# Four matmuls per block of rows: both high-part products first, then both low-part ones

## The chip, the core and the metric

The kernel runs on one core of one Trainium2 chip. The metric is the device time of one execution in microseconds (us). Most of the work is matrix multiplication on TensorE; ScalarE (ACT in the profile) and VectorE (DVE) prepare the weights and finish results, and DMA queues bring the weights from memory.

## What is computed

Two transformer blocks run on 256 tokens of 2048 features, all in float32. The first has gated linear attention, a gated convolution and a feed-forward layer; the second has a layer of pooled features and one of attention with low-rank keys and queries. Nearly all of the arithmetic is products of the activations with weight matrices:

```python
proj = jnp.einsum('bsd,dn->bsn', h, w_in[l])
...
x = x + jnp.einsum('bsd,de->bse', merged, w_o[l])
h2 = rms_norm(x, g_ffn[l])
hid = jnp.square(jax.nn.relu(jnp.einsum('bsd,df->bsf', h2, w_ffn_up[l])))
x = x + jnp.einsum('bsf,fd->bsd', hid, w_ffn_down[l])
```

## The kernel before

The activations are kept transposed, features on the 128 partitions and the 256 tokens along the free dimension. To multiply in float32 precision with the faster float32r type, each operand is written as a sum of two float32r parts, a high one and a low one. The product is taken as high x high, plus high weight x low activation, plus low weight x high activation.

Weights stream in blocks of 1 MB, in an order written out by hand (`weight_order`, L58). Each block is two units of 512 KB. For each unit `ensure` (L254) issues one ScalarE instruction that writes the high part `wh` and one VectorE instruction that writes the low part `wl`, three units ahead of their use (`NLOOK`); the next block's DMA is issued on SP's queue. At the end of each unit `end_unit` (L324) lets small tasks step: evacuation of finished sums, norms, attention pieces. Those tasks bring their own small matmuls, which stand between units on TensorE.

The function `group` (L358) is where most matmuls come from. It computes 512 output columns: two PSUM tiles, each with two feature tiles of 128 columns, and for each feature tile the 256 tokens twice, side by side: one half collects the products with the high activations (and later the low weights), the other those with the low activations. A unit holds four blocks of 128 rows (`k`, 0 to 3) of the weights for two feature tiles (`f`, 0 and 1). For each `k` and `f` the loop issues a long matmul (stationary `wh`, moving 512 columns: both parts of the activations) and a short one (stationary `wl`, moving 256 columns: the high part alone), each with its own weight load (LDWEIGHTS). So a unit has 8 long and 8 short matmuls. The helper `mm` (L227) records every matmul, so all of them carry line L230.

Three places do similar work and are not edited: the branch of `group` for a single block of 512 rows (`n == 1`, three short matmuls for each `k` and `f`), `group_tok` (L419, tokens on the partitions, where the weights are the moving operand, all matmuls 512 columns) and `narrow` (L438, one block of 128 columns).

Of the kernel before, what the change touches and what calls it, by code (L numbers as in the profile page):

```python
# [18 lines left out]
P = 128  # L19
# [38 lines left out]
def weight_order():  # L58
    """The order in which 1 MB weight blocks are used: (array, group of output columns, block of rows)."""
    out = []  # L60

    def add(name, groups, kbs=range(NKB)):
        for g in groups:
            out.extend((name, g, kb) for kb in kbs)

    add("q", range(2))
    add("lr", [0], [0])
    add("k", range(2))
    add("v", range(4))
    for g in range(4):  # L70
        for name in ("cc", "cx", "cb"):
            add(name, [g])
    for g in range(4):
        add("gb", [g])
        add("conv_out", [g])
    add("r", range(4))
    for g in range(4):
        add("ga", [g])
        add("gla_out", [g])
    add("o", range(4))  # L80
    for part in range(4):
        add("up", range(4 * part, 4 * part + 4))
        add("down", range(4), range(4 * part, 4 * part + 4))
    for half in range(2):
        for gi in (2 * half, 2 * half + 1):
            add("u", (2 * gi, 2 * gi + 1))
            add("pgate", (2 * gi, 2 * gi + 1))
            add("pgroup", (2 * gi, 2 * gi + 1), range(2))
        add("pout", range(4), range(4 * half, 4 * half + 4))
    add("kva", [0])  # L90
    add("kvr", [0], [0])
    add("qa", [0])
    for name, g in MLA:
        add(name, [g], range(NKB) if name == "bgate" else [0])
    add("bout", range(4))
    return out
# [3 lines left out]
def kernel(  # L100
# [29 lines left out]

    # ---------------------------------------------------------------- storage
    class Slot:
        """A tile in one of a fixed number of equal places, held until free()."""

# [42 lines left out]

    # ---------------------------------------------------------------- short names
    def wide(r, n=4):
        return r.unsqueeze(1).to_broadcast([r.shape[0], n, r.shape[-1]])  # L180

    # Estimated work given to each engine so far, in ns: paces the tasks between the units.
    spent = {"PE": 0.0, "DVE": 0.0, "ACT": 0.0}
# [47 lines left out]

    # ---------------------------------------------------------------- weight stream
    order = weight_order()
# [20 lines left out]
    def ensure(u, between=None):  # L254
        """Split the weights up to unit u into two float32r parts whose sum is the float32 value."""
        while state["split"] <= min(u, len(units) - 1):
# [18 lines left out]

    # ---------------------------------------------------------------- tasks between the units
    tasks = []
# [57 lines left out]
    class Out:  # L335
        """A result in SBUF, complete after `left` calls of put()."""

# [20 lines left out]
    def group(name, g, rhs, kbs=range(NKB), into=None):  # L358
        """The 512 output columns of group g, [128 features, 4, 256 tokens]: two PSUM tiles of 2 feature tiles,
        with the products of the two parts of the activations side by side. The sum of the parts goes to a slot,  # L360
        or, feature tile by feature tile, to into(ps, first feature tile)."""
        kbs = list(kbs)
# [24 lines left out]
        for e, (sb, i) in enumerate(seq):  # L387
            if sb not in acc:
                acc[sb] = psum_now("main", (P, 2, 2, T))
            ps = acc[sb]  # L390
            wh, wl = next_unit(name, g, kbs[e // 2])
            x = rhs(i)
            for k in range(4):
                first, last = i == 0 and k == 0, i == n - 1 and k == 3
                for f in range(2):
                    cs = slice(f * P, (f + 1) * P)
                    mm(ps[:, f], wh[:, k, cs], x[k // 2][:, k % 2], first, False)
                    mm(ps[:, f, 0, :], wl[:, k, cs], x[k // 2][:, k % 2, 0, :], False, last)
            end_unit()
            if i == n - 1:  # L400
                def fold(ps=ps, sb=sb):
                    fs = slice(2 * sb, 2 * sb + 2)
                    if into is None:
                        out.put(lambda s: fold_parts(s[:, fs, :], ps))
                    else:
                        out.put(lambda s: into(ps, fs))
                    ps.done()

                if into is not None:
                    out.make = lambda: 0  # L410
                defer(fold)
# [7 lines left out]
    def group_tok(name, g, rhs, kbs=range(NKB)):  # L419
        """PSUM tile [128 tokens, 2, 512 features]: the same product, tokens on the partitions."""  # L420
        ps = psum_now("main", (P, 2, 512))
# [16 lines left out]
    def narrow(name, rhs):  # L438
        """Row tile [128 features, 256 tokens] of one 128-column block."""
        ps = psum_now("misc", (P, 1, 2, T))  # L440
# [16 lines left out]

    # ---------------------------------------------------------------- splits and norms
    class Pair:
        """Groups of 4 feature tiles as two float32r parts whose sum is the float32 value: a group is two slots  # L460
        [128, feature tile, part, 256]."""

# [10 lines left out]
        def halves(self, i):  # L473
            """(feature tiles, high part, high part as float32, low part) of each slot."""
            return [(slice(2 * a, 2 * a + 2), s[:, :, 0, :], s.t.bitcast(F32)[:, :, 0, :], s[:, :, 1, :])
# [25 lines left out]
    class SumSq:  # L501
        """Sum of squares over 4 feature tiles at a time, still one for each partition."""

# [35 lines left out]
    def rstd_steps(out, m, mean_plus_eps):  # L539
        """out = 1 / sqrt(m), m already holding the mean plus eps; one Newton step."""  # L540
        mean_plus_eps()
# [8 lines left out]
    def spread(out, c):  # L550
        """out[p, t] = c[t]: the column [128 tokens, 2] as a row on all partitions."""
        dg = row("dg")
# [10 lines left out]
    def token_sums(ss):  # L563
        """PSUM [128 tokens, 2]: the sums of squares of the tokens."""
        tot = ss.fold()
# [8 lines left out]
    def rms_steps(ss, n, out, c):  # L574
        """The norm's factor of each token, as a column c and as a row out."""
        ps = yield from token_sums(ss)
# [13 lines left out]

    # ---------------------------------------------------------------- constants
    ones = const.tile([P, P], F32, name="ones")
# [26 lines left out]
    rows = {}  # L619
# [3 lines left out]

    # ================================================================ first block
    h = Pair(4)
# [33 lines left out]
    def decay(ps_lr):  # L659
        """log of the decay of each token and key feature, summed within blocks of 128 tokens."""  # L660
        wg = slot("wg", (P, 1024))
# [32 lines left out]

    # scores of the gated linear attention, a level of the token tree at a time
    ST = []
# [136 lines left out]

    # gated convolution
    cbu = Pair(4)
# [96 lines left out]
    for n in ("R16", "R2"):  # L932
        rows.pop(n).free()
    # the residual stream again
    xs = [slot("x") for _ in range(4)]
# [29 lines left out]

    # feed-forward
    gfa = const.tile([P, 16], F32, name="gfa")
# [33 lines left out]
    def two_norms():  # L1001
        """The final norm of the first block, then the first norm of the second on its result."""
        r1, r2 = row("R1"), row("R12")
# [32 lines left out]

    # ================================================================ second block
    hkv, hb = Pair(4), Pair(4)
# [20 lines left out]
    def pool_evac(ps, gi, n, pooled):  # L1059
        """Mean over the last tokens, less the token itself."""  # L1060
        while "R12" not in rows:
# [58 lines left out]

    # rotary tables
    trig = [row("C"), row("S")]
# [27 lines left out]

    # keys, values, queries
    rope_task = spawn(rope_tables())
# [19 lines left out]
    def rope_rows(out, raw, n):  # L1172
        """raw: [128, n, 256], two heads of 64 features on the partitions."""
        ps = yield from psum_later("misc", (P, n, T))
# [131 lines left out]
    def attend(hq):  # L1306
# [6 lines left out]
        begun[hq] = state["unit"]  # L1313
        # factor of the scores: 192^-0.5 times the norm of the queries
        rq = rows["Cq"]
# [115 lines left out]

# [1 line left out]
def _blocks(name, w):  # L1433
    """[K, N] -> [N/512, K/512, 128, 2048]: 1 MB blocks of two units, in the order of their use."""
    K, N = w.shape
# [14 lines left out]
def _narrow(w):  # L1450
    """[2048, 128] -> [1, 1, 128, 16 * 128]."""
    return np.ascontiguousarray(w.reshape(16, P, P).transpose(1, 0, 2)).reshape(1, 1, P, 2048)
# [98 lines left out]
```

## Time and profile before

| What | Value |
|---|---|
| time, median of 3 runs | 2790.2 us (2789.09 to 2792.19) |
| span of the profiled execution | 2789.3 us |
| TensorE matmul busy | 2776.8 us, 15,906 instructions |
| VectorE busy | 1788.2 us |
| ScalarE busy | 1345.4 us |
| DMA | 511.69 MB, mean 183 GB/s |

The span reaches from the first to the last instruction of one profiled execution; the page gives no further time for that execution, and the span lies inside the range of the timed runs. Matmuls are pipelined: the profile's duration of a matmul (0.39 us for 512 columns) is longer than the distance from its start to the next one's start, so distances of starts, not durations, tell how fast TensorE goes. The starts are shown in steps of 10 ns.

### The profile page before, as it was taken

The numbers are of one execution on the slowest core, as the hardware profiler recorded it, in microseconds if no ns is written. First come the engines' busy times: TensorE is split into PE (matmuls) and PEld (weight loads), VectorE is DVE, ScalarE is ACT, GpSimd is POOL, SyncE is SP. The second block draws the span as 40 slices with busy tenths as digits, with TensorE's granted clock in tenths as the row PEclk, the third lists the DMA queues.
The fourth block names the chain that finished last, engine by engine and source line by source line (L and its number), as shares of the span: only waits on it lengthen the run. The fifth ranks groups of instructions, "written<-read, shape, count | busy, mean of one in ns | idle before, by whom it ended". The sixth has DMA issues, their size and how long they took to land.

```text
span 2789.3 us, 38593 instructions
## 1 busy us (share of the span) xinstructions
PE 2776.8 (100%) x15906; PEld 2417.8 (87%) x15906; DVE 1788.2 (64%) x2119; ACT 1345.4 (48%) x1584; POOL 25.9 (1%) x36
## 2 busy tenths in 40 slices
PE   8999999999999999999999999999999999999999
PEld 7888888888888888888888888888888888899788
DVE  6676666655665666656566566687657677767464
ACT  5644444544554444434344345554434445555563
POOL 0000000000000000000000000000000000000000
PEclk9999999999999999999999999999999999999999
DMA  6444455555555655554545555555555555545244
GB/s 249 174 150 152 167 180 191 187 195 184 195 185 193 221 187 184 193 183 181 196 173 193 192 182 184 190 192 182 187 190 181 183 194 196 198 174 189 91 167 150
DMA packets 73712, 511.69 MB, mean 183 GB/s; under 512 B 8208, under 2 KB 8752, under 8 KB 13248
## 3 DMA queue, kind: packets, MB, share of 16 engines
q1 hardware_dynamic: 72496, 506.94, 51.6%
q8 instruction: 124, 2.03, 0.3%
q10 hardware_dynamic: 1040, 2.29, 0.2%
q14 instruction: 52, 0.43, 0.0%
HBM read 504.99 MB, written 4.21 MB: 183 GB/s over the span
## 4 chain that ended last, share of the span: by engine, by line
PE 99%; DVE 0%; DMA 0%; ACT 0%; issue 0%; SPq 0%; DVEq 0%; ACTq 0%
PE main L230 96%; PE misc L230 2%; DMA raw<-w_q_dram 0%; PE misc L1374 0%; DVE wl L193 0%; DVE cum L683 0%; ACT e L225 0%; ACT wh L225 0%; SPq L246 0%; ACT ls L225 0%; DVE x L193 0%; ACT L225 0%; DVE ls L206 0%; DVE out L193 0%; PE misc L1241 0%
## 5 line engine op out<-in xcount | busy, mean ns | idle before, releaser
L230 PE MATMUL main<-part,wh 128*128 128x512 f32 (+1 forms) x7360 | 2540.8, 392 | 6.5 <-ACT wh L225 6.5
L230 PE MATMUL main<-part,wl 128*128 128x256 f32 x7200 | 2021.3, 281 | 0.9 <-DVE wl L193 0.8
L193 DVE TENSOR_TENSOR wl<-raw,wh 128x1024 fp32r<-128x1024 f32 (+1 forms) x946 | 1152.5, 1221 | 954.5 <-ACT wh L225 950.1
L230 PEld LDWEIGHTS main<-part,wh 128*128 128x128 f32 x7360 | 1372.2, 188 | 324.1 <-ACT wh L225 6.9
L225 ACT ACTIVATE wh<-raw 128x1024 fp32r<-128x1024 f32 (+1 forms) x946 | 996.4, 1057 | 1214.7 <-PE main L230 1119.9
L230 PEld LDWEIGHTS main<-part,wl 128*128 128x128 f32 x7200 | 1361.9, 189 | 2.3 <-DVE wl L193 2.0
L193 DVE TENSOR_TENSOR out<-main,out 128x512 f32<-128x512 f32 x164 | 112.1, 684 | 8.2 <-ACT out L225 8.2
L230 PE MATMUL main<-wh,part 128*128 128x512 f32 x320 | 105.4, 400 | 0.0
L225 ACT ACTIVATE out<-main 128x512 f32<-128x512 f32 x164 | 94.8, 579 | 0.0
L193 DVE TENSOR_TENSOR x<-main,x 128x512 f32<-128x512 f32 x128 | 88.0, 688 | 9.7 <-PE main L230 7.5
L230 PEld LDWEIGHTS main<-wh,part 128*128 128x128 f32 x320 | 60.8, 190 | 12.8 <-issue 0.3
L230 PE MATMUL main<-wl,part 128*128 128x512 f32 x160 | 62.9, 393 | 0.0
L225 ACT ACTIVATE part<-out 128x512 fp32r<-128x512 f32 x56 | 33.2, 627 | 50.8 <-DVE out L206 44.2
L193 DVE TENSOR_TENSOR out<-out,R 128x1024 f32<-128x1024 f32 x42 | 51.5, 1226 | 1.4
L225 ACT ACTIVATE Z<-Z 128x1024 f32<-128x1024 f32 x16 | 17.0, 1061 | 41.9 <-DVE Z L193 36.9
L193 DVE TENSOR_TENSOR part<-out,part 128x512 fp32r<-128x512 f32 x56 | 36.2, 687 | 0.5
L230 PEld LDWEIGHTS main<-wl,part 128*128 128x128 f32 x160 | 30.5, 191 | 5.9
L225 ACT ACT_TABLE_LOAD x24 | 30.8, 1283 | 1.1 <-PEq L1540 0.7
L206 DVE SCALAR_TENSOR_TENSOR part<-x,vec,part 128x256 fp32r<-128x256 f32 x64 | 26.8, 479 | 5.4 <-ACT part L225 5.4
L1068 POOL COPY s<-out 128x4 f32<-128x4 f32 x8 | 9.5, 1188 | 2222.8 <-ACT wh L225 1818.3
L230 PEld LDWEIGHTS misc<-Z 128*128 128x128 f32 x240 | 29.0, 191 | 1.1
L225 ACT ACTIVATE part<-x,vec 128x256 fp32r<-128x256 f32 x64 | 27.2, 496 | 2.8 <-DMA x<-xT 2.8
(188 smaller groups left out, 826.1 us busy)
## 6 DMA issues: line engine op xcount, KB each, us to landing
raw<-w_up_dram SPq DMA_DIRECT2D x64, 1024.0 KB, 4.8
raw<-w_down_dram SPq DMA_DIRECT2D x64, 1024.0 KB, 4.8
raw<-w_u_dram SPq DMA_DIRECT2D x32, 1024.0 KB, 4.8
raw<-w_pgate_dram SPq DMA_DIRECT2D x32, 1024.0 KB, 4.8
raw<-w_pout_dram SPq DMA_DIRECT2D x32, 1024.0 KB, 4.8
raw<-w_v_dram SPq DMA_DIRECT2D x16, 1024.0 KB, 4.8
raw<-w_cc_dram SPq DMA_DIRECT2D x16, 1024.0 KB, 4.8
raw<-w_cx_dram SPq DMA_DIRECT2D x16, 1024.0 KB, 4.9
```

Source lines behind the costliest of these rows:

```text
L193: nc.vector.tensor_tensor(out, a, b, op)
L206: nc.vector.scalar_tensor_tensor(out, a, s, b, op0, op1)
L225: nc.scalar.activation(out, a, f, bias=bias, scale=scale, **kw)
L230: nc.tensor.matmul(out, lhsT, rhs, start=start, stop=stop, skip_group_check=True)
L1068: nc.gpsimd.tensor_copy(nx[:, :, 0:d], cur[:, :, 0:d])
```

## The change

For each block of 128 rows the loop over the two feature tiles is split in two. Before, the order is: long and short of feature tile 0, long and short of feature tile 1. After, it is: long of tile 0, long of tile 1, short of tile 0, short of tile 1. Operands, destinations and flags of each matmul stay the same. The rest of the diff removes comments and docstrings and keeps every line number.

```diff
             for k in range(4):
                 first, last = i == 0 and k == 0, i == n - 1 and k == 3
                 for f in range(2):
-                    cs = slice(f * P, (f + 1) * P)
-                    mm(ps[:, f], wh[:, k, cs], x[k // 2][:, k % 2], first, False)
-                    mm(ps[:, f, 0, :], wl[:, k, cs], x[k // 2][:, k % 2, 0, :], False, last)
+                    mm(ps[:, f], wh[:, k, f * P:(f + 1) * P], x[k // 2][:, k % 2], first, False)
+                for f in range(2):
+                    mm(ps[:, f, 0, :], wl[:, k, f * P:(f + 1) * P], x[k // 2][:, k % 2, 0, :], False, last)
             end_unit()
```

## Rows read from the trace of the kernel before

**Rows 1.** The page: engines' busy time, granted TensorE clock, chain by engine.
```profile
PE 2776.8 (100%) x15906; PEld 2417.8 (87%) x15906; DVE 1788.2 (64%) x2119; ACT 1345.4 (48%) x1584; POOL 25.9 (1%) x36
...
PEclk9999999999999999999999999999999999999999
...
PE 99%; DVE 0%; DMA 0%; ACT 0%; issue 0%; SPq 0%; DVEq 0%; ACTq 0%
```

**Rows 2.** Waits, whole span: who for whom, us, times, longest.
```profile
ACT wh L225 <- PE main L230: 1119.9, 727, 3.5
...
PE main L230 <- ACT wh L225: 6.5, 2, 6.4
...
PE main L230 <- DVE wl L193: 0.8, 1, 0.8
```

**Rows 3.** TensorE's groups by shape: count, busy us, mean ns, idle before.
```profile
L230 PE MATMUL main<-part,wh 128*128 128x512 f32 x7040 | 2481.1, 397 | 6.5 <-ACT wh L225 6.5
L230 PE MATMUL main<-part,wl 128*128 128x256 f32 x7200 | 2021.3, 281 | 0.9 <-DVE wl L193 0.8
L230 PE MATMUL main<-wh,part 128*128 128x512 f32 x320 | 105.4, 400 | 0.0
L230 PE MATMUL main<-wl,part 128*128 128x512 f32 x160 | 62.9, 393 | 0.0
L230 PE MATMUL main<-part,wh 128*128 128x256 f32 x320 | 59.8, 289 | 0.0
...
L230 PE MATMUL misc<-part,wh 128*128 128x512 f32 x32 | 11.4, 399 | 0.0
```

**Rows 4.** Chain in order of time, pieces of matmuls: start, us, matmuls.
```profile
285.66 25.08 PE main L230 x144
...
396.82 662.83 PE main L230 x3824
...
1071.83 717.97 PE main L230 x4064
1790.13 11.21 PE main L230 x64
...
1825.11 596.42 PE main L230 x3376
...
2681.90 102.38 PE main L230 x592
```

**Rows 5.** Timeline of TensorE around 1790 us: start, duration, instruction.
```profile
1788.57 0.40 PE L230 MATMUL main<-part,wh 128*128 128x512 f32 x1
1788.81 0.28 PE L230 MATMUL main<-part,wl 128*128 128x256 f32 x1
1788.93 0.40 PE L230 MATMUL main<-part,wh 128*128 128x512 f32 x1
...
1789.63 0.50 PE L230 MATMUL misc<-ones,sq 128*128 128x1 f32 x4
...
1790.78 0.39 PE L230 MATMUL main<-part,wh 128*128 128x512 f32 x1
1791.01 0.28 PE L230 MATMUL main<-part,wl 128*128 128x256 f32 x1
1791.13 0.39 PE L230 MATMUL main<-part,wh 128*128 128x512 f32 x1
```

**Rows 6.** Timeline of TensorE at 905 us, in the first long piece.
```profile
905.22 0.39 PE L230 MATMUL main<-part,wh 128*128 128x512 f32 x1
905.45 0.28 PE L230 MATMUL main<-part,wl 128*128 128x256 f32 x1
905.57 0.39 PE L230 MATMUL main<-part,wh 128*128 128x512 f32 x1
```

**Rows 7.** Timeline of TensorE at 1305 us, in the second long piece.
```profile
1305.21 0.40 PE L230 MATMUL main<-part,wh 128*128 128x512 f32 x1
1305.45 0.28 PE L230 MATMUL main<-part,wl 128*128 128x256 f32 x1
1305.57 0.40 PE L230 MATMUL main<-part,wh 128*128 128x512 f32 x1
1305.81 0.28 PE L230 MATMUL main<-part,wl 128*128 128x256 f32 x1
1305.92 0.40 PE L230 MATMUL main<-part,wh 128*128 128x512 f32 x1
1306.16 0.28 PE L230 MATMUL main<-part,wl 128*128 128x256 f32 x1
1306.27 0.40 PE L230 MATMUL main<-part,wh 128*128 128x512 f32 x1
```

**Rows 8.** Timeline, token-major helper, settled; between the two rows nine matmuls start.
```profile
2575.09 0.62 PE L230 MATMUL main<-wh,part 128*128 128x512 f32 x2
...
2577.13 0.62 PE L230 MATMUL main<-wh,part 128*128 128x512 f32 x2
```

**Rows 9.** Timeline, token-major helper after an interruption; three matmuls from row to row.
```profile
145.86 0.39 PE L230 MATMUL main<-wl,part 128*128 128x512 f32 x1
...
147.94 0.39 PE L230 MATMUL main<-wl,part 128*128 128x512 f32 x1
...
148.62 0.39 PE L230 MATMUL main<-wl,part 128*128 128x512 f32 x1
```

**Rows 10.** Timeline, branch with one block of rows; first and last of 21 distances.
```profile
2534.90 0.29 PE L230 MATMUL main<-part,wl 128*128 128x256 f32 x1
...
2537.42 0.28 PE L230 MATMUL main<-part,wl 128*128 128x256 f32 x1
```

**Rows 11.** Timeline at the start of the kernel, with the idle time before.
```profile
14.50 0.49 PE L230 MATMUL main<-part,wh 128*128 128x512 f32 x1 [0.18 <-ACT wh L225]
15.76 0.39 PE L230 MATMUL main<-part,wl 128*128 128x256 f32 x1 [0.77 <-DVE wl L193]
```

## The prediction

> **What bounds the kernel now.** I read the page's engine line and its chain first. TensorE is busy for 2776.8 of 2789.3 us, the chain that ended last is 99% TensorE, and the granted clock stands in the top tenth in all 40 slices; VectorE has 64% and ScalarE 48% [rows 1]. The table of waits agrees: matmuls waited 6.5 us for ScalarE's split and 0.8 us for VectorE's in the whole execution, while ScalarE waited 1119.9 us for TensorE [rows 2]. So no transfer and no other engine sets the pace. The time is the count of matmuls times the distance from the start of one to the start of the next, and only a change of that distance can move it.
>
> The groups by shape show whose distance it is [rows 3]. The loop that is edited issues 7,040 long matmuls (512 columns, high weight part) and 7,040 short ones (256 columns, low part; of the 7,200 shown, 160 belong to the branch with one block of rows, which isn't edited). That is 7,040 pairs, or 3,520 quads of two feature tiles. The `narrow` helper's 32 pairs, the token-major helper's 480 long matmuls and that branch's 480 short ones keep their order.
>
> The chain in order of time then shows something that the busy shares hide. In its long unbroken pieces the same pair of matmuls has two speeds [rows 4]. From 396.82 us, 3,824 matmuls took 662.83 us: 346.7 ns a pair. From 1071.83 us, 4,064 took 717.97 us, and from 1825.11 us, 3,376 took 596.42 us: 353.3 ns a pair both times. The piece from 2681.90 us, 592 in 102.38 us, is back at 346. I call these the quick and the slow rhythm. A stretch keeps its rhythm until some other matmul breaks in: four one-column matmuls stand between slow pairs at 1788 us and quick ones at 1791 us [rows 5]. The four pieces hold 11,856 matmuls, 2,964 quads, in 2079.6 us, so a quad costs 701.6 ns now; 3,720 of their 5,928 pairs run slow. The other 1,112 pairs lie in short blocks, such as 64 matmuls in 11.21 us or 144 in 25.08 us, 350.3 and 348.3 ns a pair.
>
> **The change part by part.** It removes nothing and adds nothing: 14,080 matmuls and weight loads of the same shapes, the same unit ends, the same tasks between units, no DMA and no queue touched. What it alters is which matmul follows which. Now there are two kinds of neighbour, long to short and short to long. Afterwards there are four in each quad: long to long, long to short, short to short, short to long.
>
> *Long to short and short to long.* In the quick rhythm the starts are 230 ns and about 117 ns apart [rows 6]. In the slow one a round of three pairs takes 1.06 us, with 240 ns behind every long matmul and 110 to 120 ns behind every short one [rows 7]. So, to the 10 ns of this view, the whole slow price, 353.3 - 346.7 = 6.6 ns a pair, stands behind the long matmul that a short one follows.
>
> *Long to long.* The edited loop has none, so I take the token-major helper, whose matmuls are all long though with the roles of weights and activations exchanged. Settled, 9 of them go from 2575.09 to 2577.13 us, 226.7 ns each [rows 8]. After an interruption, 9 go from 145.86 to 147.94 us, 231.1 ns each, and then they settle by themselves, at 0.68 us for three [rows 9]. So 227 is the lower bound and 231 the upper one; the value is 227, because the stream leaves its slow state within about ten matmuls.
>
> *Short to short.* The branch with one block of rows shows it: 21 from 2534.90 to 2537.42 us, 120.0 ns each [rows 10]. Its third matmul changes from high to low weights as here. The two rhythms show no second level in this row.
>
> A quick quad is then 226.7 + 230 + 120 + 116.7 = 693.4 ns, which is exactly two quick pairs (2 x 346.7). The reorder by itself gives nothing: each matmul seems to cost its columns and a fixed surplus. In the slow rhythm the price stands behind a long matmul followed by a short one, and a quad has one such place where it had two: 693.4 + 6.6 = 700.0 ns against 706.6. This is the gain I forecast.
>
> The Trainium skill ("TensorE: Matmul & The Clock Gate", section on the back-to-back issue gap) gives a gap that depends on the matmul's own columns alone, columns over 2.4 GHz plus about 2.5 ns. By it a quad is 650 ns in either order and the change moves nothing. The trace measures 693 to 707 ns instead, so the surplus is larger than the page's and, in the slow rhythm, not a function of the columns alone.
>
> *Waits and releases.* The low part's first use moves from the second matmul of a unit to the third. VectorE's wait of 0.77 us before one low-part matmul at 15.76 us [rows 11] can shrink by about one long matmul, 0.23 us; bounds 0 and 0.8 us (all waits for it), value 0.3. The high part's last use moves one short matmul earlier in the unit, 0.12 us in some 2.8, so ScalarE's split may start that much sooner; ScalarE is 48% busy and waits on TensorE anyway, so this is worth nothing. If the cover went, a late split would appear as a matmul wait, of which there are 7.3 us now. The two PSUM halves of a tile take turns one matmul later than before; in rows 8 three matmuls in a row meet the same half, then the other, at one even distance, so I cost this at nothing.
>
> **Sum.** With the present share of slow stretches, 3,720 / 2 = 1,860 slow quads x 6.6 ns = 12.3 us, plus 0.3 us at the start; the short blocks are left alone. 2789.3 - 12.6 = 2776.7 us of span. The page gives the span of the profiled execution; it is 0.9 us under the median of 2790.2, and I carry that over: 2778 us (2777.6), 0.4% faster. About 0.2%, or 5.6 us, is what a measurement of this kernel can tell from no change.
>
> **Rivals.**
> 1. *All quick.* The long-to-long step pulls every quad into the quick rhythm as it does the token-major stream. Steady quads gain (701.6 - 693.4) x 2,964 = 24.3 us, short blocks at most 350.3 - 346.7 = 3.6 ns x 1,112 = 4.0 us: 2790.2 - 28.3 = 2762 us. For it: rows 9 settling. Against it: only two long ones follow each other, while rows 9 needed some nine.
> 2. *Nothing.* The surplus belongs to each matmul and the rhythm to the engine's phase, at full price whatever follows; the share of slow stretches stays. Then 701.6 ns a quad remain and the time is 2790 us. For it: the quick quad and two quick pairs have the same sum. The Trainium skill's rule above stands on this side too. Against it: rows 7 put the price in one kind of neighbour.
> 3. *Slow everywhere* (the other side). The quad brings a rhythm of its own, in which the unsettled long-to-long step (231) and the slow long-to-short step (240) both recur: 231 + 240 + 120 + 114 = 705 to 707 ns in every stretch, never broken, because two short matmuls undo what two long ones settle. Price: (706.6 - 701.6) x 2,964 = 14.8 us and up to 353.3 - 350.3 = 3.0 ns x 1,112 = 3.3 us in the short blocks: 2790.2 + 18.1 = 2808 us. It decides as soon as the mean steady quad exceeds 701.6 ns. For it: today's slow rhythm lasts for hundreds of us unless something breaks in. Against it: half of the stretches need no such rhythm today.
>
> **How the numbers follow.** Forecast (2770 to 2784): 0.36. All quick (2758 to 2770): 0.16. Nothing (2785 to 2796): 0.22. Slow (2796 to 2810): 0.26. So faster by over 0.2% is 0.36 + 0.16 = 0.52, within it 0.22, slower 0.26. The forecast's own range is 2770 to 2784 us. For 8 in 10 the range must reach both outer rivals: 2759 to 2806 us, leaving out the tails of each.
>
> **What would show it.** Right: in the chain's long pieces a quad takes 693 or 700 ns, the starts inside a quad are about 227, 230 to 237, 120 and 117 ns apart, the waits for splits stay under 8 us. The forecast is wrong if slow stretches stand at 707 (rival 2 or 3), if all stand at 693 (rival 1), or if short to short exceeds 120 ns, which adds 3.5 us for each nanosecond. Waits of matmuls on ScalarE or VectorE beyond today's would mean that the splits had become the bound, which none of these steps expects.

## The result, and the profile after

The changed kernel takes 2773.6 us (median of 4 runs, 2772.1 to 2777.3); the kernel before took 2790.8 us beside it. The ratio is 0.9940, with a 95% interval of 0.9926 to 0.9954: 0.6% faster. The profiled execution spans 2771.9 us, against 2789.3.

The page of the changed kernel shows that nothing else changed hands. TensorE still runs the same 15,906 matmuls through the whole span at the same granted clock, and the chain is TensorE's:

```profile
PE 2759.3 (100%) x15906; PEld 2403.6 (87%) x15906; DVE 1787.4 (64%) x2119; ACT 1346.4 (49%) x1584; POOL 25.7 (1%) x36
...
PEclk9999999999999999999999999999999999999999
...
PE 99%; DVE 0%; DMA 0%; ACT 0%; issue 0%; SPq 0%; DVEq 0%; ACTq 0%
```

Neither did the waits of the matmuls (who waits for whom, us in total, times, longest), which answer to [rows 2]:

```profile
PE main L230 <- ACT wh L225: 6.9, 2, 6.3
PE main L230 <- DVE wl L193: 0.5, 1, 0.5
```

The one wait that the new order could shorten did shorten: before the first low-part matmul of the third unit 0.53 us are idle, against 0.77 [rows 11]. This is the timeline of TensorE at the start:

```profile
15.86 0.50 PE L230 MATMUL main<-part,wl 128*128 128x256 f32 x2 [0.53 <-DVE wl L193]
```

The time came out of the long pieces of matmuls. The chain in order of time (start, us, matmuls) of the changed kernel:

```profile
284.78 24.91 PE main L230 x144
...
395.58 666.01 PE main L230 x3824
...
1073.61 707.81 PE main L230 x4064
1781.76 11.25 PE main L230 x64
...
1816.61 587.98 PE main L230 x3376
...
2664.13 102.79 PE main L230 x592
```

Set beside [rows 4], with the same counts of matmuls: the piece that was quick became 3.2 us longer (662.83 to 666.01), the two slow ones 10.2 and 8.4 us shorter, the last one 0.4 us longer. That is 15.0 of the 17.4 us; of the rest, 1.2 us were gained before the first long piece and 0.8 us between the third and the last. Divide each by its quads: 666.01 / 956, 707.81 / 1,016 and 587.98 / 844 are all 696.7 ns. The last piece can't be divided like that, before or after: 32 of its 592 matmuls are attention's own, in two blocks of 16 that the chain counts in. Here is the first block:

```profile
2666.76 2.78 PE L230 MATMUL main<-pt,v 128*128 128x256 f32 x16
```

Behind the second block the starts give 348.3 ns a pair, 696.7 ns a quad, as elsewhere. Before, the quads were at 693.3 and at 706.6. So the changed order has one speed in all long pieces, between the two of the old order and nearer to the quick one.

Inside a piece (timeline of TensorE at 1305 us; two matmuls of a kind in one row), two long matmuls take 0.46 to 0.47 us and two short ones 0.23, and two quads go from 1304.74 to 1306.13 us:

```profile
1304.74 0.63 PE L230 MATMUL main<-part,wh 128*128 128x512 f32 x2
1305.20 0.39 PE L230 MATMUL main<-part,wl 128*128 128x256 f32 x2
1305.43 0.62 PE L230 MATMUL main<-part,wh 128*128 128x512 f32 x2
1305.90 0.40 PE L230 MATMUL main<-part,wl 128*128 128x256 f32 x2
1306.13 0.63 PE L230 MATMUL main<-part,wh 128*128 128x512 f32 x2
```

### The profile page after: what moved, and what is told of

The parts are those of the page before. It is cut to its first block, busy times and chain, and to the rows that moved or that the text cites. A ratio compares the mean times of both kernels' runs of the same rounds, so it can differ in the third digit from the quotient of the medians.

```text
span 2771.9 us, 38593 instructions
## 1 busy us (share of the span) xinstructions
PE 2759.3 (100%) x15906; PEld 2403.6 (87%) x15906; DVE 1787.4 (64%) x2119; ACT 1346.4 (49%) x1584; POOL 25.7 (1%) x36
## 4 chain that ended last, share of the span: by engine, by line
PE 99%; DVE 0%; DMA 0%; ACT 0%; issue 0%; SPq 0%; DVEq 0%; ACTq 0%
PE main L230 96%; PE misc L230 2%; DMA raw<-w_q_dram 0%; PE misc L1374 0%; DVE wl L193 0%; DVE cum L683 0%; ACT e L225 0%; ACT wh L225 0%; SPq L246 0%; ACT ls L225 0%; DVE x L193 0%; ACT L225 0%; DVE ls L206 0%; DVE out L193 0%; PE misc L1241 0%
## 5 line engine op out<-in xcount | busy, mean ns | idle before, releaser
L230 PE MATMUL main<-part,wh 128*128 128x512 f32 (+1 forms) x7360 | 2278.5, 392 | 6.9 <-ACT wh L225 6.9
L230 PE MATMUL main<-part,wl 128*128 128x256 f32 x7200 | 1430.2, 278 | 0.7 <-DVE wl L193 0.5
L230 PEld LDWEIGHTS main<-part,wh 128*128 128x128 f32 x7360 | 1124.0, 189 | 11.4 <-ACT wh L225 7.1
L230 PE MATMUL misc<-Z 128*128 128x64 f32 (+1 forms) x240 | 28.6, 271 | 0.0
```

The lines of the kernel that those rows point to most:

```text
L230: nc.tensor.matmul(out, lhsT, rhs, start=start, stop=stop, skip_group_check=True)
```

## The experiments

Four theories were set against each other. N (neighbours) is the prediction's: which length follows which sets the distance of two starts. P (PSUM halves; a half is here the part of a PSUM tile that belongs to one feature tile): the old order writes the same half of the PSUM tile twice in a row, the new one never does, and that is the gain. R (rhythm): every repeating sequence of matmuls falls into a rhythm of its own, picked where a stretch restarts after an interruption and kept until the next. S (stage): data, addresses or the stage of the kernel decide which stretch is slow.

**Longer groups.** All long matmuls of a unit, then all short ones:

```diff
-            for k in range(4):
-                for f in range(2): long(k, f)
-                for f in range(2): short(k, f)
+            for k, f in kf: long(k, f)
+            for k, f in kf: short(k, f)
```

Here `long` and `short` stand for the two `mm` lines of the loop, and `kf` for the eight pairs in the loop's order. All runs below keep each matmul's operands and flags.

> Per unit all 8 long matmuls, then all 8 short ones (as the changed kernel, with the group spread from one block of rows to four). Theory N (the distance of two starts is set by which length follows which): 14 of 16 neighbours are now of equal length, whose settled distances are 227 and 120 ns; four times 693 ns a unit, 2762 to 2767 us. Theory P (the gain came from successive matmuls no longer writing the same PSUM half): the halves alternate just as in the changed kernel, so 2774 us. Theory R (every repeating sequence falls into a rhythm of its own, which no sum of neighbours gives): anywhere from 693 to 707 ns per four matmuls, 2762 to 2808 us, but one value in all long pieces.

Measured: 2778.6 us, ratio 0.9956 (0.9943 to 0.9968). N (2762 to 2767 us) and P (2774 us) both miss. The chain has one value again, as R has it, 698.3 ns for four matmuls in each piece (667.61 / 956, 709.51 / 1,016):

```profile
395.17 667.61 PE main L230 x3824
...
1074.83 709.51 PE main L230 x4064
...
1819.63 589.39 PE main L230 x3376
```

The timeline shows why long runs don't reach the 227 ns of [rows 8]: eight short ones take 0.95 us (119 ns each), eight long ones 1.84 us, 230 each. The long ones settle as in [rows 9], but in each unit anew: averaged by place over the units between 500 and 1000 us of the trace, their first five distances lie between 228 and 236 ns, the last three at 226.7.

```profile
905.24 1.11 PE L230 MATMUL main<-part,wl 128*128 128x256 f32 x8
906.19 2.00 PE L230 MATMUL main<-part,wh 128*128 128x512 f32 x8
908.03 0.64 PE L230 MATMUL main<-part,wl 128*128 128x256 f32 x4
```

**Groups of four.** The same with two blocks of rows at a time, four long and four short.

```diff
+            for k in (0, 2):
+                for j in (k, k + 1): long(j, 0); long(j, 1)
+                for j in (k, k + 1): short(j, 0); short(j, 1)
```

> Four long, then four short matmuls (two blocks of rows together). Theory N: between the changed kernel and the run with whole units, about 2768 us. Theory P: 2774 us, as the halves still alternate. Theory R: one value for all long pieces, somewhere between 693 and 707 ns per four matmuls, not ordered by the length of the group.

Measured: 2789.8 us, ratio 0.9995 (0.9986 to 1.0004), no gain at all. One value in all long pieces, 701.6 to 701.7 ns (670.77 / 956, 712.88 / 1,016). Groups of two, four and eight give 696.7, 701.7 and 698.3 ns: not in the order of their length. Theory N is out with this run, for it wanted a time between the other two. P misses again: the halves alternate here at every step as in the changed order, and the gain is gone.

```profile
396.35 670.77 PE main L230 x3824
...
1079.21 712.88 PE main L230 x4064
```

**PSUM halves.** First the changed order with the two long ones exchanged, so that two of four neighbours meet the same half:

```diff
-                long(k, 0); long(k, 1); short(k, 0); short(k, 1)
+                long(k, 1); long(k, 0); short(k, 0); short(k, 1)
```

> Long of tile 1, long of tile 0, short of tile 0, short of tile 1: the lengths follow each other as in the changed kernel, but two of four neighbours write the same PSUM half. Theory N and theory R: 2774 us, and 696 to 697 ns per four matmuls as in the changed kernel. Theory P: about half of the gain is lost, some 2782 us.

Measured: 2774.1 us, ratio 0.9941 (0.9928 to 0.9953), and the long pieces last 666.01, 707.81 and 587.98 us, to the last digit those of the changed kernel. Then the old alternation of long and short, with each short one a pair later. This was meant to keep neighbours from ever meeting the same half, and it doesn't: each `short(*a)` differs from the `long(*b)` before it, but the next `long` writes the half of that short one again. Written out, 6 of the 16 steps of a unit stay in one half, against 8 in the old order and none in the changed one.

```diff
+            long(*kf[0])
+            for a, b in zip(kf, kf[1:]):
+                long(*b)
+                short(*a)
+            short(*kf[-1])
```

> Long and short alternate as before the change, but each short one comes one pair later, so that no two successive matmuls write the same PSUM half (at the two ends of a unit two long and two short ones meet). Theory N: inside the unit the neighbours are those of the kernel before, so about 2790 us, with pairs of 347 and of 353 ns in different pieces. Theory P: 2774 us or less, with no slow piece. Theory R: two rhythms again or one, between 2762 and 2800 us; the two meetings per unit may break a slow rhythm up.

Measured: 2800.5 us, ratio 1.0035 (1.0023 to 1.0048), slower than before, with one value of 705 ns in the long pieces:

```profile
397.26 673.93 PE main L230 x3824
...
1083.32 716.23 PE main L230 x4064
...
1835.04 595.01 PE main L230 x3376
```

Theory P is out on both counts, but by other runs than this one: meeting the same half costs nothing (the exchanged long ones), and never meeting it is no gain by itself (groups of four, 2789.8 us). The lagging order can't test P. N expected two speeds here and misses too: there is one, and a bad one. Whether the odd turns at the ends of a unit make it or the lag itself was not separated.

**Is the slow rhythm a matter of chance?** The kernel before, profiled a second time:

> The kernel before once more, unchanged, for a second profile. Theory R with the program's own interruptions setting the moment of restart: the same pieces quick and slow, 663, 718 and 596 us long to within 0.1 us. If the rhythm were picked by chance in each execution, pieces would change places between 346.7 and 353.3 ns a pair, by 13.5, 12.7 and 11.2 us.

One run, 2794.2 us. The three pieces last 662.83, 717.97 and 596.42 us, as in [rows 4] to the last digit. So the rhythm is not drawn anew in each execution; something that both executions share picks it. This execution's span is 3.1 us longer for other reasons: the first long piece starts 1.5 us later (the granted clock averaged 0.91 over the first 20 us; in the first profile it was 1.00 there, the level of 2.4 GHz), and 1.7 us more pass between the third long piece and the last.

```profile
398.30 662.83 PE main L230 x3824
...
1073.30 717.97 PE main L230 x4064
...
1826.59 596.42 PE main L230 x3376
...
2685.04 102.38 PE main L230 x592
```

**Interruptions put in.** The kernel before, and then the changed one, with one to four one-column matmuls at every 48th unit (the profile shows each such float32 matmul as two records, so the four records in [rows 5] are two matmuls):

```diff
             end_unit()
+            if state["unit"] % 48 == 7:
+                nudge()      # 1 + n % 4 times matmul(ps[:, 0:1], ones, ones[:, 0:1]) into a free PSUM tile
```

> The kernel before, with 1 to 4 one-column matmuls (into an unused PSUM tile, read by nobody) put between two units at every 48th unit; each such interruption costs about 0.3 to 0.6 us, some 18 of them 5 to 10 us. Theory R (a stretch falls into the quick or the slow rhythm at the moment it restarts, and keeps it): the unbroken pieces of before split into stretches of both kinds, the slow one also in the piece from 397 us, the quick one also in those from 1072 and 1825 us; total between 2772 and 2815 us, by the shares. Theory S (the data, addresses or stage decide): after every interruption the piece returns to the rhythm that it has in the kernel before; about 2797 us.

Measured: 2794.6 us, ratio 1.0008 (0.9999 to 1.0017). The total says little; the chain says all. Between two interruptions lie 768 matmuls, and they take either 133.23 or 135.79 us, in what were single pieces:

```profile
481.72 133.23 PE main L230 x768
615.07 135.79 PE main L230 x768
751.19 133.23 PE main L230 x768
884.99 135.79 PE main L230 x768
...
1155.80 133.24 PE main L230 x768
1289.38 135.79 PE main L230 x768
1425.73 135.79 PE main L230 x768
1562.30 133.23 PE main L230 x768
```

The difference is 2.56 us over 384 pairs, 6.7 ns a pair: the two rhythms, turning both ways within one stage of the kernel and on the same kind of data. Theory S is out, and R is shown for the old order. After four matmuls the next long stretch was quick each of four times. After three it was slow three times, and quick once, before the last 400 matmuls (the row below). There the pairs last 343 or 344 and 350 ns in turn by the starts: a third pattern, with the quick mean of 346.7. After one or two both came.

```profile
2717.02 69.46 PE main L230 x400
```

> The same interruptions in the changed kernel. Theory R with only one stable rhythm for this order: every stretch is back at 696.7 ns per four matmuls within a few dozen, and the time is that of the changed kernel plus the interruptions' own 5 to 10 us, 2779 to 2784 us. If the changed order also has a slow rhythm that its restarts happened to miss, some stretches show another value, 700 or more, and the time is above 2784 us.

Measured: 2784.9 us, ratio 0.9972 (0.9962 to 0.9982). Every stretch of 768 takes 133.87 or 133.88 us. The changed order falls back into the same rhythm after each interruption that was tried. The time lies just above the range expected, because the span grew by 11.9 us (2783.8 - 2771.9) with 18 interruptions, 0.66 us for each, and not by the 5 to 10 us assumed; what two executions differ by anyway is in that number.

```profile
481.31 133.87 PE main L230 x768
615.30 133.87 PE main L230 x768
749.50 133.87 PE main L230 x768
883.94 133.87 PE main L230 x768
...
1556.73 133.88 PE main L230 x768
```

**Each order where it was best.** The old order up to the feed-forward layer, the new one from there:

```diff
+                if state["unit"] < FIRST:    # first unit of "up"
+                    ...  # long(k, 0); short(k, 0); long(k, 1); short(k, 1)
+                else:
+                    ...  # long(k, 0); long(k, 1); short(k, 0); short(k, 1)
```

> The old order up to the first unit of the feed-forward layer, where its long piece was quick (346.7 ns a pair), the new order from there on. Theory R: the first long piece takes 662.8 us again instead of 666.0, the later ones 707.8 and 588.0 as in the changed kernel; short blocks early on lose what the new order gave them, up to 2 us; about 2772 us. If the new order's gain came from the waits of the split or from anything spread evenly over the units, the first part would lose 0.6% of its 1060 us instead, 2780 us.

Measured: 2773.1 us, ratio 0.9931 (0.9919 to 0.9944). The long pieces last as R says, 662.92, 707.81 and 587.98 us. Against the changed kernel the gain is within what can be told from no change, since the early short blocks lost part of the 3.1 us again (the piece now starts at 396.61 us, against 395.58).

**The old order, kicked.** If the restart picks the rhythm, two interruptions in the right places should be worth more than the reorder. The kernel before with four one-column matmuls at two places:

```diff
             end_unit()
+            if state["unit"] - FIRST in (12, 280):    # 13, 281 and 14, 282 in the other two runs
+                nudge()      # four one-column matmuls
```

> The order before, with four one-column matmuls (unused PSUM tile) put between two units at two places only, shortly after the starts of the pieces that ran slow (1072 and 1825 us). Each costs about 0.8 us. Theory R: where the restart leads to the quick rhythm the rest of the piece loses 6.6 ns a pair, some 13 us in the first and 10 us in the second; both quick: 2768 to 2770 us, one quick: 2779 to 2782 us, none: 2793 us. In the run with interruptions at every 48th unit, four one-column matmuls were followed by the quick rhythm each time. Theory S is already out.

> The same, both interruptions one unit later. A unit has 8 pairs and the slow rhythm repeats after 3, so the restart falls at another point of the round. If the point of the round at the restart decides, the three runs may differ, each 2769, 2781 or 2793 us; if four one-column matmuls always lead to the quick rhythm, all three are at 2768 to 2770 us.

> The same, both interruptions two units later than in the first of the three. As there: 2769, 2781 or 2793 us if the point of the round decides, 2768 to 2770 us if the four matmuls alone do.

Measured: 2768.4, 2769.0 and 2769.6 us; ratios 0.9918 (0.9904 to 0.9931), 0.9919 and 0.9919 (both 0.9905 to 0.9932). All three are quick in all long pieces. The chain of the first:

```profile
396.85 662.83 PE main L230 x3824
...
1078.30 698.99 PE main L230 x4032
...
1824.43 574.19 PE main L230 x3312
...
2659.24 102.38 PE main L230 x592
```

698.99 us for 2,016 pairs and 574.19 for 1,656 are 346.7 ns a pair. The trace shows the slow round still running just before each kick. Moved by one unit or two, the kick still works, so four matmuls alone suffice there. Their runs (2766.5 to 2769.9 us) lie below all runs of the changed kernel (2772.1 to 2777.3), though the two were not timed side by side. This is the fastest version found: the old order, 16 more records on TensorE, 0.8% less time. The timeline shows the price of one kick, from 1077.35 to 1078.16 us:

```profile
1077.00 0.40 PE L230 MATMUL main<-part,wh 128*128 128x512 f32 x1
1077.23 0.28 PE L230 MATMUL main<-part,wl 128*128 128x256 f32 x1
1077.35 0.95 PE L362 MATMUL misc<-ones 128*128 128x1 f32 x8
1078.16 0.48 PE L230 MATMUL main<-part,wh 128*128 128x512 f32 x1
```

## Why the prediction was right, and where it was not

- *What bounds the kernel*: right. The same matmuls at the same clock, the waits as small as before, and 15.0 of the 17.4 us in the distance of starts in the long pieces.
- *Two rhythms in the old order, kept until something breaks in*: right, and now shown by [rows 4] coming back to the digit in a second execution and by stretches that turn both ways when interrupted.
- *The price stands in the old slow rhythm and the reorder recovers part of it*: right in sign and near in sum, the sum by luck. The forecast was 2778 us; 2773.6 lies in the range that it gave the forecast alone (2770 to 2784). But its own sign, long pieces at 693 or 700 ns a quad, did not come: none of them ran at either. By the shares it used, the two average 697.5 ns, and that lies near the one value measured, 696.7.
- *The step that failed* is "a quad has one such place where it had two", and the term built on it, "1,860 slow quads x 6.6 ns = 12.3 us". It carried the two rhythms of the old order into the new one, as 693.4 and 700.0 ns. The runs show a rhythm of the new order's own instead, a single one of 696.7 ns. The 1,860 formerly slow quads gained 10.0 ns each (10.2 + 8.4 = 18.6 us), and the 1,096 quick ones, which were to lose nothing, lost 3.3 (3.2 + 0.4 = 3.6 us): 15.0 us instead of 12.3. The other 2.4 us are short blocks and the start, which the sum left alone but for 0.3 us.
- *The terms inside a quad* were not right one by one. Averaged over the starts between 500 and 1000 us of the changed kernel's trace, long to long takes 232.9 ns (put at 226.7, at most 231), long to short 233.3 (230 quick, 236.6 slow), short to short 114.6 (120) and short to long 115.8 (116.7). Errors of opposite sign left a sum near the truth. That lengths of neighbours set the distance (theory N), which carried those terms, failed in the runs with groups of four and eight and with the lagging short ones.
- *Rows misread, without weight for the sum*: the four records in [rows 5] are two matmuls. The last piece of [rows 4] holds 560 matmuls of the loop, not 592. And the 350.3 ns of a short block hold the end of its last matmul; inside the block at 1790 us the starts give the quick 346.7. So the short-block terms of the rivals (4.0 and 3.3 us) were not sound.
- *PSUM halves and waits costed at nothing*: right. Exchanging the long ones changed no digit of the long pieces; the wait at the start shrank by 0.24 us, 0.3 expected.
- *The rivals*: "nothing" is out, since the price changed with the order. "All quick" didn't happen with this order, but its time, 2762 us, is not far from what the old order reached with two kicks, 2768 to 2770 us. "Slow everywhere" did not happen at its price of 705 to 707 ns, yet its picture came nearest: the quad has a rhythm of its own in every long piece, and its long-to-long step stays unsettled. Another order, with lagging short ones, does run at 705 ns.

The Trainium skill's rule for the gap of two matmuls ("TensorE: Matmul & The Clock Gate", section on the back-to-back issue gap) gives, as an estimate, 650 ns for a quad in any order. The section calls this the gap of isolated matmuls and says that in a stream of weight loads and matmuls both set the spacing, which the prediction left out. The orders tried here measure 693 to 707, so the estimate lay below all of them.

What stays open is why the rhythms exist. No run shows what inside TensorE, or between it and its memories, the starts fall in step with; the weight load before each matmul, for one, was never varied. Nor is it known what in an interruption picks the rhythm. Whether some interruption would put the changed order into another rhythm was tried only with one to four one-column matmuls at 18 places.

## What to carry to other kernels

Where a kernel is bound by back-to-back matmuls, divide the long pieces of the chain by their counts, after a look at whether other matmuls are counted in. If the same sequence has two speeds without waits and at the same granted clock, put a tiny interruption into a slow piece: when the speed changes behind it, the gap was a rhythm of the starts, and it is worth the difference times the count. In this kernel an order of matmuls could not be costed from distances taken from other orders; a per cent either way had to be measured, and the order in which one rhythm was found is safer than the one with two. The interruption can be worth more than a reorder, but what follows it was not always the same (after one, two or three matmuls both rhythms came), so it must be looked for again after each edit.

## What the runs showed of the hardware

All steady periods found here, each taken as the repeat that the starts show, are whole multiples of 6.67 ns, to 0.2 ns: the quick pair 346.7 ns (52), the slow round of three pairs 1060 (159), two quads of the changed order 1393.3 (666.01 us / 478; 209), a unit with groups of eight 2793.3 (667.61 / 239; 419), with groups of four 2806.6 (670.77 / 239; 421), two units with lagging short ones 5640.0 (by the starts; 846). What has that step wasn't found. At a granted clock of 0.998 or 0.999 the same four matmuls differ by 1.9% between the rhythms (693.3 against 706.6 ns), and whole kernels by 1.2% (2768.4 us with the kicks against 2800.5).
